# Two gate tiles taken from the attention pools' buffers, and the T4 products of the first two column blocks put ahead of both T1 products

## The chip, the cores and the metric

The kernel runs on one core of a Trainium2 chip. A core has a matrix engine (TensorE: PE in the profile, and PEld for its weight loads), VectorE (DVE), ScalarE (ACT), GpSimd (POOL) and SyncE (SP), each with its own in-order stream of instructions, and DMA queues that move data between the chip's memory and the on-chip buffers. The metric is the time of one execution of the whole program on the device, in microseconds (us), smaller being better.

## The reference

One block of a hybrid network, batch 1, 1024 tokens, width 1024, all in float32:

```python
mod = jax.nn.silu(c) @ w_mod[l] + b_mod[l]
u = modulate(rms_norm(h, ln1_g[l]), shift1, scale1)
# token_mixer(u):
proj = u @ w_in
p_fox, p_rwkv, p_gate = _split(proj, (FOX_COLS, RWKV_COLS, GATE_COLS))
...   # o_fox: causal attention, 8 heads of 64, with a forget-gate bias on the logits
...   # o_rwkv: a linear recurrence over the tokens, 8 heads of 64
gate_fox, gate_rwkv = jnp.split(jax.nn.sigmoid(p_gate), N_BRANCHES, axis=-1)
merged = gate_fox * (o_fox @ fox_w_out) + gate_rwkv * (o_rwkv @ rwkv_w_out)
mix = merged @ w_o
...
h = h + gate1[:, None, :] * mix
u2 = modulate(rms_norm(h, ln2_g[l]), shift2, scale2)
# conv_ffn(u2):
a, b = jnp.split(u @ w_up, 2, axis=-1)      # 2 x 2816 columns
a = lax.conv_general_dilated(a, ...) + conv_b   # width 3, causal, each channel by itself
h = h + gate2[:, None, :] * ((jax.nn.silu(a) * b) @ w_down)
return rms_norm(h, final_g)
```

The change touches two places of it: `sigmoid(p_gate)`, and the product `u @ w_up`.

## The kernel before

Every product of float32 matrices is made as three products of a faster matrix format (float32r): a high part (ACT rounds the number, a CAST) and a low part (DVE subtracts the high part from it) stand for each operand, and hi·hi, hi·lo and lo·hi are added up in one accumulator bank of 128x512 numbers. There are eight such banks.

The program goes through stages: the modulation and norm, the recurrence (with the projections and most gates woven between its steps), the attention, the two branch products and the output product (`br`, `wo`), the up product, the down product (`D`). On PE the program's text sets the order. On ACT, DVE and SP it is the text's order inside `manual_schedule` stretches (the attention, and the up product from its second tokens' half on); outside them a scheduler orders the instructions by its own estimate of when each can start. So in the recurrence's tail the order on ACT, DVE and SP follows from what the scheduler believes each instruction waits for.

**The gates.** `gate_steps` (L327) works out 128 gate columns for 1024 tokens in two halves of 512. A half is 24 matmuls into a bank `gt`, then on ACT Abs (L337), Exp (L338) and Ln (L339), on DVE one instruction (L340) that reads the bank once more, on ACT Exp (L341), and on SP a store to `d_gate` (L342). Everything works in one buffer `gs`. That buffer comes from the pool `gsp` (tag `sp0`, two buffers, used in turn), so that the Abs of a half must wait until the store of the half before the last has left the buffer. The bank comes from the pool `pb` (tag `big`, two banks, in turn): the bank of a half is free when its L340 is done. The halves of gate 8 are called `gs8_0` and `gs8_1` here, their banks `gt8_0` and `gt8_1`; they are the only ones that stand in the program between the opening of the attention's pools and the attention.

At L987 the pools of the attention open: `at` with the heads' operands (`stA`, `stB`, `vh`, which POOL loads at L995 to L999), the probabilities `P` (four buffers) and the short probabilities `Ps` (two buffers, 128x512, for the first four row blocks of a head), and banks. `load_head(0)` starts the first head's loads. Then `weave.step()` runs what is left of gate 8, and the attention begins. From there a gate goes another way (`late_gate`, L1134): all of its halves share one bank, `rk_ps`, which is the second of the two next banks of `pb`; a half is 24 matmuls, then Abs (L1162) and Relu (L1163) on ACT, after which the bank is free for the next half's matmuls. In the program's order `rk_ps` takes the bank that `gt8_0` had. Gate 9's first half comes right behind `gt8_1` on PE, gate 9's second half is interleaved with the first logits `lg`.

**The up product.** It is made for blocks i of 128 columns of each of the two parts (22 of them), by a scheme with seven half-size products instead of eight. Product k of block i, (i, k) below, multiplies one combination of weights by one combination of tokens, 12 matmuls:

```python
OPS = {1: ("A11", "B11"), 2: ("A12", "B21"), 3: ("S4", "B22"), 4: ("A22", "T4"), 5: ("S1", "T1"), 6: ("S2", "T2"),
       7: ("S3", "T3")}
```

Products 1, 6, 5, 3 of a block accumulate in one bank `X`, products 7 and 4 in a bank `Y`. What a bank holds in between is used too: after (i, 4) DVE adds `Y` to `U` (L1564), after (i, 5) it adds `X` to `Z` (L1566, into `Ze_a` for the first two blocks), and only then may (i, 3) go on in `X`. The list `plan` is the order of the products on PE, and also the order in which `up_ahead` makes the weights' operands (a CAST at L1481 and a subtraction at L1485 each), four to six products ahead. The tokens' combinations are made in between, in the text's order: T2 behind the first four products, then T4 (L1750), T1 (L1754) and the high and low parts of B22 (L1722, L1724), each combination as four casts and four subtractions of 128x512. The sums for S4 stand at L1477, two instructions before S4's subtraction on DVE. What the products leave is fetched by `up_evac`, called in the order of `plan`.

Of the kernel before, what the change touches and what calls it, by code (L numbers as in the profile page):

```python
# [9 lines left out]
F32 = mybir.dt.float32  # L10
# [8 lines left out]
NH = 512  # L19
# [113 lines left out]
def hybrid_block(ctx: ExitStack, tc: tile.TileContext, a, out):  # L133
# [110 lines left out]
    marks = {}  # L244
# [40 lines left out]
    def gemm_steps(ps, w, x, cs, nk=KT, w0=0, by_kt=False):  # L285
        (wh, wl), (xh, xl) = w, x
        order = [(i, kt) for i in range(3) for kt in range(nk)]
        if by_kt:
            order.sort(key=lambda o: o[1])
        for n, (i, kt) in enumerate(order):  # L290
            ww, xx = ((wh, xh), (wh, xl), (wl, xh))[i]
            k0 = (w0 + kt) * 128
            mm(ps, ww[:, k0 : k0 + 128], xx[:, kt, cs], start=n == 0, stop=n == len(order) - 1)
            yield
# [32 lines left out]
    def gate_steps(w, i, pps, ptag, pool, tag):  # L327
        if weave.late == 1:
            yield from late_gate(w, i)
            return  # L330
        for hf in range(2):
            cs = slice(hf * NH, hf * NH + NH)
            ps = pps.tile([128, NH], F32, tag=ptag, name=f"gt{i}_{hf}")
            yield from gemm_steps(ps, w, u, cs)

            g = pool.tile([128, NH], F32, tag=tag, name=f"gs{i}_{hf}")
            nc.scalar.activation(g, ps, AF.Abs)  # L337
            nc.scalar.activation(g, g, AF.Exp, scale=-1.0)  # L338
            nc.scalar.activation(g, g, AF.Ln, bias=1.0)  # L339
            stt(g, ps, 0.0, g, op0=ALU.min, op1=ALU.subtract)  # L340
            nc.scalar.activation(g, g, AF.Exp)  # L341
            nc.sync.dma_start(d_gate[i, :, cs], g)  # L342
# [3 lines left out]
    with ExitStack() as es:  # L346
# [613 lines left out]
        for i in range(16):  # L960
            weave.add(lambda i=i: w_in(26 + i), lambda w, i=i: gate_steps(w, i, pb, "big", gsp, "sp0"))
# [26 lines left out]
    at = es.enter_context(tc.tile_pool(name="at", bufs=2, reuse_waits="tile"))  # L988
# [4 lines left out]
    def load_head(h):  # L993
        A = at.tile([128, 2, S], F32R, tag="stA", name=f"stA{h}")
        nc.gpsimd.dma_start(A, d_st[h, 0:2, :, :].rearrange("k r s -> r k s"))  # L995
        B = at.tile([128, 2, S], F32R, tag="stB", name=f"stB{h}")
        nc.gpsimd.dma_start(B[0:68, :, :], d_st[h, 2:4, 0:68, :].rearrange("k r s -> r k s"))
        vh = at.tile([128, 8, 128], F32R, tag="vh", name=f"vh{h}")
        i = nc.gpsimd.dma_start(vh, d_v[h])  # L999
        marks.setdefault("head", i)  # L1000
        heads[h] = A, B, vh

    load_head(0)
    while len(weave.queue) > 12:
        weave.step()
    fx = [[fxp.tile([128, S], F32R, tag=f"h{4 * x + p}", name=f"fx{x}{p}") for p in range(4)] for x in range(2)]
# [3 lines left out]
    with tc.manual_schedule(engines={mybir.EngineType.DVE, mybir.EngineType.Activation}):  # L1010
# [129 lines left out]
        def late_gate(w, i):  # L1140
            while any(x[1] is w[1] for x in late_lo):
                for _ in lower():
                    pass
            for hf in range(2):
                cs = slice(hf * NH, hf * NH + NH)
                yield from gemm_steps(rk_ps, w, u, cs)
                if i == 15 and hf == 1:

                    marks["rest"] = rk_ps
                    return  # L1150
                weave.hold = weave.now + 1000
                pending.append((i, hf))
                weave.spawn(gate_out(i, hf, cs), 260)
                yield
# [76 lines left out]
    if "rest" in marks:  # L1231
        g, m = (gsp.tile([128, NH], F32, tag="sp0", name=f"rest{k}") for k in range(2))
        i = nc.scalar.activation(g, marks["rest"], AF.Abs)
# [89 lines left out]
    for x in range(2):  # L1323
        for n in range(8):
            if x or n:
                k = 8 * x + n + 1
# [277 lines left out]
        put(6, s1[:, NH:])  # L1604

    plan = [(i, k) for ks in ((1, 2), (7,), (6,)) for i in range(2) for k in ks]
    plan += [(0, 4), (0, 5), (1, 5), (1, 4), (0, 3), (1, 3)] + [(2, k) for k in (1, 7, 6, 2, 4, 5)]
    for i in range(3, NFF):
        plan += [(i, 1), (i, 7), (i - 1, 3)] + [(i, k) for k in ((6, 2, 4, 5) if i < NFF - 1 else (6, 2, 5, 4))]
    plan.append((NFF - 1, 3))  # L1610
# [427 lines left out]
```

## Time and profile before

| | us |
|---|---|
| median of 3 runs | 1646.45 (1645.22 to 1648.16) |
| the profiled execution | 1648.91, its span 1647.1 |
| PE busy | 1607.8 (98% of the span) |
| DVE busy | 1222.6 (74%) |
| ACT busy | 820.9 (50%) |
| POOL busy | 130.8 (8%) |

The span is the time from the first to the last recorded instruction; the execution's own time is 1.8 us more. A row of the timeline has the start, the duration, the engine, the line, what is written and what is read, the shapes and the count of merged instructions, and in brackets how long the engine had been idle and whom it waited for. A matmul's recorded duration (0.39 us) is longer than the distance to the next one (0.227 us), since they overlap. The stage borders used below: the attention starts at about 622 us, the up product at about 1000 us, its regular part at 1054 us, the down product at 1430 us.

### The profile page before, as it was taken

The page shows a single profiled execution, that of the slowest core. Times are in us where ns is not written, and L with a number is a line of the kernel's source. Part 1 is how long each engine was busy: PE and PEld are TensorE (multiplying, and loading weights), DVE is VectorE, ACT ScalarE, POOL GpSimd, SP SyncE. Part 2 cuts the span into 40 slices and gives each one's busy share as a digit, 9 for nine tenths or more (in the row PEclk, how much of TensorE's full clock was granted, in tenths as well). Part 3 has the DMA queues.
Part 4 walks back from the last instruction along what each step waited for, and adds up shares of the span by engine and source line. Part 5 has one row for each costly group of instructions (what it writes and reads, how often), then busy time and mean ns, then how long its engine had stood idle before and what let it go on. Part 6 is the DMA issues. An engine that isn't in the chain of part 4 may idle for free.

```text
span 1647.1 us, 25947 instructions
## 1 busy us (share of the span) xinstructions
PE 1607.8 (98%) x9694; PEld 1339.6 (81%) x9694; DVE 1222.6 (74%) x2373; ACT 820.9 (50%) x1537; POOL 130.8 (8%) x153
## 2 busy tenths in 40 slices
PE   7999999999999999999999999999999999999998
PEld 7777788798978788888888888788888888888886
DVE  5786787878876526888679447887777777886677
ACT  5563335445445646766623235644444444555455
POOL 0011101111111010221022000000000000000000
PEclk9999999999999999999999999999999999999999
DMA  8488645543332346433197420242232232675363
GB/s 339 138 326 242 178 123 143 134 123 94 107 115 85 97 126 157 129 117 106 56 353 270 168 81 26 84 134 97 96 119 98 96 109 96 225 254 160 122 211 109
DMA packets 121645, 240.59 MB, mean 146 GB/s; under 512 B 40048, under 2 KB 48880, under 8 KB 121520
## 3 DMA queue, kind: packets, MB, share of 16 engines
q1 hardware_dynamic: 113040, 220.58, 41.0%
q0 software_dynamic: 8480, 18.37, 4.2%
q8 instruction: 76, 1.25, 0.3%
q14 instruction: 49, 0.40, 0.1%
HBM read 173.35 MB, written 65.54 MB: 145 GB/s over the span
## 4 chain that ended last, share of the span: by engine, by line
PE 58%; DVE 5%; ACT 2%; DMA 2%; issue 1%; SPq 0%; ACTq 0%; DVEq 0%
PE X L141 13%; PE D L141 13%; PE Y L141 6%; PE wo L141 5%; PE br L141 4%; PE rk_ps L141 3%; PE W L141 3%; PE gt L141 3%; PE lg L141 2%; PE ov L141 2%; PE tp L145 2%; DMA d_gate<-gs 1%; DVE nm L1049 1%; DVE P L1059 1%; DVE tl L1089 0%
## 5 line engine op out<-in xcount | busy, mean ns | idle before, releaser
L141 PE MATMUL D<-op,op 128*128 128x512 f32 x924 | 209.8, 389 | 0.0
L141 PEld LDWEIGHTS D<-op,op 128*128 128x128 f32 x924 | 173.3, 188 | 36.3 <-DVE op L1261 0.3
L141 PE MATMUL X<-T_m,S 128*128 128x512 f32 x440 | 107.8, 390 | 1.6 <-ACT T_m L1722 1.1
L141 PEld LDWEIGHTS X<-T_m,S 128*128 128x128 f32 x440 | 82.4, 188 | 20.4 <-ACT T_m L1722 2.5
L1260 ACT CAST op<-g 128x512 fp32r<-128x512 f32 x77 | 47.8, 621 | 73.8 <-PE D L141 49.0
L1261 DVE TENSOR_TENSOR op<-g,op 128x512 fp32r<-128x512 f32 x77 | 53.0, 688 | 41.4 <-ACT op L1260 41.4
L1519 DVE SCALAR_TENSOR_TENSOR c<-ab,vec,c 128x512 f32<-128x512 f32 x88 | 65.9, 750 | 18.4 <-ACT c L1522 16.8
L784 DVE TENSOR_TENSOR t<-E,M 128x60 f32<-128x60 f32 (+24 forms) x248 | 55.6, 224 | 27.9 <-DMA M<-sm 21.8
L1485 DVE TENSOR_TENSOR A<-ur,A 128x512 fp32r<-128x512 f32 x64 | 44.0, 688 | 38.7 <-ACT A L1481 38.5
L1485 DVE TENSOR_TENSOR S<-ur,S 128x512 fp32r<-128x512 f32 x66 | 45.5, 691 | 35.2 <-ACT S L1481 35.1
L274 DVE TENSOR_TENSOR lo_in<-raw_in,hi_in 128x512 fp32r<-128x512 f32 x84 | 56.7, 712 | 17.6 <-PE gt L141 4.8
L1481 ACT CAST S<-ur 128x512 fp32r<-128x512 f32 x66 | 41.0, 622 | 55.8 <-DVE ur L1474 30.6
L141 PE MATMUL Y<-T_h,S 128*128 128x512 f32 x264 | 63.6, 390 | 0.4 <-ACT T_h L1740 0.4
L141 PE MATMUL Y<-T_h,A 128*128 128x512 f32 x264 | 63.7, 389 | 0.3 <-ACT T_h L1722 0.3
L1053 ACT ACTIVATE P<-lg,nm 128x896 f32<-128x896 f32 (+3 forms) x64 | 47.4, 743 | 30.7 <-DVE nm L1049 22.5
L1481 ACT CAST A<-ur 128x512 fp32r<-128x512 f32 x64 | 39.6, 622 | 43.1 <-PE X L141 31.3
L786 DVE TENSOR_TENSOR E<-E,t 128x60 f32<-128x60 f32 (+24 forms) x248 | 56.2, 227 | 6.4
L141 PE MATMUL W<-B_f,A 128*128 128x512 f32 x252 | 60.6, 389 | 0.0
L141 PE MATMUL X<-B_b,A 128*128 128x512 f32 x252 | 60.5, 389 | 0.0
L141 PEld LDWEIGHTS Y<-T_h,S 128*128 128x128 f32 x264 | 49.5, 188 | 11.1 <-ACT T_h L1740 0.8
L141 PEld LDWEIGHTS Y<-T_h,A 128*128 128x128 f32 x264 | 49.5, 188 | 10.9 <-ACT T_h L1722 0.7
L272 ACT CAST hi_in<-raw_in 128x1024 fp32r<-128x1024 f32 x42 | 43.8, 1048 | 26.3 <-PE ps_rkv L141 11.3
(483 smaller groups left out, 4134.4 us busy)
## 6 DMA issues: line engine op xcount, KB each, us to landing
raw_in<-in_w_in SPq DMA_DIRECT2D x50, 512.0 KB, 4.0
wm<-in_w_mod SPq DMA_DIRECT2D x48, 512.0 KB, 7.3
ur<-in_w_up SPq DMA_DIRECT2D x44, 512.0 KB, 3.8
g<-d_g SPq DMA_DIRECT2D x35, 512.0 KB, 4.0
d_g<-gs SPq DMA_DIRECT2D x44, 256.0 KB, 2.0
d_g<-c SPq DMA_DIRECT2D x33, 256.0 KB, 4.4
d_st<-qh SPq DMA_DIRECT2D x64, 128.0 KB, 2.5
stA<-d_st POOLq DMA_DIRECT2D x8, 1024.0 KB, 6.9
```

The source lines that it names most:

```text
L141: nc.tensor.matmul(o, lhsT, rhs, start=start, stop=stop, skip_group_check=more)
L145: nc.tensor.transpose(o, i, eye)
L272: nc.scalar.copy(hi, raw)
L274: nc.vector.tensor_tensor(lo[:, c : c + NH], raw[:, c : c + NH], f32(hi[:, c : c + NH]), op=ALU.subtract)
L784: tt(tv, E32[:, 0:J, s : s + 1].to_broadcast([128, J, W]), M32[:, s : s + 1, s + 1 : 32].to_broadcast([128, J, W]), op=ALU.mult)
L786: tt(E32[:, 0:J, s + 1 : 32], E32[:, 0:J, s + 1 : 32], tv, op=ALU.add)
L1053: nc.scalar.activation(e[:, 0:n], lg[:, 0:n], AF.Exp, bias=nm[:, 0:1], accum_out=nm[:, 1:2])
L1260: nc.scalar.copy(hi, src)
L1261: tt(lo, src, f32(hi), op=ALU.subtract)
L1481: nc.scalar.copy(hi, src)
L1485: tt(lo, src, f32(hi), op=ALU.subtract)
L1519: stt(c, ab[:, x + hf * NH : x + hf * NH + NH], V("conv_w", 22 * x + i), c, op0=ALU.mult, op1=ALU.add)
```

## The change

Three lines of code move. A gate's buffer `gs` comes from the attention's pool, tag `Ps`, if that pool is open (only the two halves of gate 8 meet this). And in the list `plan` the product (1, 4) moves from behind (1, 5) to a place right behind (0, 4).

```diff
@@ gate_steps
-            g = pool.tile([128, NH], F32, tag=tag, name=f"gs{i}_{hf}")
+            g = marks["spare"].tile([128, NH], F32, tag="Ps", name=f"gs{i}_{hf}", bufs=2) if "spare" in marks else \
+                pool.tile([128, NH], F32, tag=tag, name=f"gs{i}_{hf}")
             nc.scalar.activation(g, ps, AF.Abs)
             nc.scalar.activation(g, g, AF.Exp, scale=-1.0)
             nc.scalar.activation(g, g, AF.Ln, bias=1.0)
...
     load_head(0)
+    marks["spare"] = at
     while len(weave.queue) > 12:
         weave.step()
...
-    plan += [(0, 4), (0, 5), (1, 5), (1, 4), (0, 3), (1, 3)] + [(2, k) for k in (1, 7, 6, 2, 4, 5)]
+    plan += [(0, 4), (1, 4), (0, 5), (1, 5), (0, 3), (1, 3)] + [(2, k) for k in (1, 7, 6, 2, 4, 5)]
```

Line numbers below L337 are one larger in the changed kernel from L337 on, and two larger from L1005 on.

The first place is ACT at the end of the recurrence. The scheduler orders ACT there, and with other buffers it chose another order. Before, the rows for gate 8, with the last normalisation of the recurrence (`rs`) in them:

```order
L337 ACTIVATE gs8_0_6850<-gt8_0_6777 128x512
L932 ACTIVATE rs3_1_6811<-va3_1_6786,epsr_76 128x512
L338 ACTIVATE gs8_0_6850<-gs8_0_6850 128x512
L933 ACTIVATE rs3_1_6811<-rs3_1_6811 128x512
L339 ACTIVATE gs8_0_6850<-gs8_0_6850 128x512
L341 ACTIVATE gs8_0_6850<-gs8_0_6850 128x512
L337 ACTIVATE gs8_1_6882<-gt8_1_6857 128x512
L338 ACTIVATE gs8_1_6882<-gs8_1_6882 128x512
L339 ACTIVATE gs8_1_6882<-gs8_1_6882 128x512
L341 ACTIVATE gs8_1_6882<-gs8_1_6882 128x512
L1162 ACTIVATE gs9_0_6922<-rk_ps_6892 128x512
```

And the same stretch of ACT in the changed kernel:

```order
L933 ACTIVATE rs3_1_6811<-va3_1_6786,epsr_76 128x512
L934 ACTIVATE rs3_1_6811<-rs3_1_6811 128x512
L338 ACTIVATE gs8_0_6850<-gt8_0_6777 128x512
L338 ACTIVATE gs8_1_6882<-gt8_1_6857 128x512
L339 ACTIVATE gs8_0_6850<-gs8_0_6850 128x512
L339 ACTIVATE gs8_1_6882<-gs8_1_6882 128x512
L340 ACTIVATE gs8_0_6850<-gs8_0_6850 128x512
L340 ACTIVATE gs8_1_6882<-gs8_1_6882 128x512
L342 ACTIVATE gs8_0_6850<-gs8_0_6850 128x512
L342 ACTIVATE gs8_1_6882<-gs8_1_6882 128x512
L1164 ACTIVATE gs9_0_6922<-rk_ps_6892 128x512
```

The two halves, which stood one behind the other, are now interleaved step by step: the Abs of the second half, which reads the bank `gt8_1`, stands ahead of the Exp of the first. On DVE the L340 of `gs8_0` moves behind the recurrence's last two instructions accordingly, and on SP the store of `gs8_0` moves behind the recurrence's last store. PE's order there is the same in both. The first two `Ps` probabilities now stand behind gate 8's two stores, since they use the same two buffers.

The second place is DVE in the up product, between the low parts of B22 (whose second half is the first row) and the fetch of (1, 4) or (1, 5). Before:

```order
L1724 TENSOR_TENSOR B221_m13_10937<-u21_m11_10666,B220_e3_10935 128x512 x2
L1485 TENSOR_TENSOR A22_1_10946<-ur11_10422,A22_1_10946 128x512
L1566 TENSOR_TENSOR Ze_a7_10662<-X_0_10678,Ze_a7_10662 128x512
L1477 TENSOR_TENSOR ur00_10309<-ur00_10309 128x512
L1485 TENSOR_TENSOR S4_0_10963<-ur00_10309,S4_0_10963 128x512
L1566 TENSOR_TENSOR Ze_a7_10662<-X_1_10750,Ze_a7_10662 128x512
L1477 TENSOR_TENSOR ur10_10421<-ur10_10421 128x512
L1485 TENSOR_TENSOR S4_1_10984<-ur10_10421,S4_1_10984 128x512
L1485 TENSOR_TENSOR A11_2_10986<-ur20_10966,A11_2_10986 128x512
L1564 TENSOR_TENSOR U_1_10900<-Y_1_10841,U_1_10900 128x512
```

And in the changed kernel:

```order
L1726 TENSOR_TENSOR B221_m13_10937<-u21_m11_10666,B220_e3_10935 128x512 x2
L1487 TENSOR_TENSOR S1_1_10946<-ur11_10422,S1_1_10946 128x512
L1566 TENSOR_TENSOR U_1_10900<-Y_1_10841,U_1_10900 128x512
L1479 TENSOR_TENSOR ur00_10309<-ur00_10309 128x512
L1487 TENSOR_TENSOR S4_0_10963<-ur00_10309,S4_0_10963 128x512
L1568 TENSOR_TENSOR Ze_a7_10662<-X_0_10678,Ze_a7_10662 128x512
L1479 TENSOR_TENSOR ur10_10421<-ur10_10421 128x512
L1487 TENSOR_TENSOR S4_1_10984<-ur10_10421,S4_1_10984 128x512
L1487 TENSOR_TENSOR A11_2_10986<-ur20_10966,A11_2_10986 128x512
L1568 TENSOR_TENSOR Ze_a7_10662<-X_1_10750,Ze_a7_10662 128x512
```

The three fetches have moved in a circle: the fetch of (1, 4), which stood last, now stands first, and the two fetches into `Ze_a` ((0, 5) and (1, 5)) stand one fetch later, each behind a sum and a low part for S4. The operands S1 of both blocks are made one place later and A22 of block 1 two places earlier, on ACT as on DVE.

## The prediction

> **What bounds the kernel now.** First the page's heads, then the chain that ended last, in order of time.
>
> ```profile
> span 1647.1 us, 25947 instructions
> PE 1607.8 (98%) x9694; PEld 1339.6 (81%) x9694; DVE 1222.6 (74%) x2373; ACT 820.9 (50%) x1537; POOL 130.8 (8%) x153
> ```
> ```profile
> 607.50 10.46 DMA d_gate<-gs
> ...
> 622.39 6.21 PE rk_ps L141 x19
> ...
> 1054.26 3.04 PE X L141 x12
> ...
> 1429.94 209.68 PE D L141 x924
> ```
>
> PE is busy for 98%, so only its few gaps can be won or lost. From 1054.26 us on the chain is PE alone, to the end: what PE is late by there, the program is late by. One long piece ahead of that isn't PE: a gate store of 10.46 us. The timeline around it (gate 8, then gate 9 in `rk_ps`):
>
> ```profile
> 609.14 0.60 ACT L337 ACTIVATE gs<-gt 128x512 f32<-128x512 f32 x1 [1.66 <-PE gt L141]
> 609.63 0.68 ACT L932 ACTIVATE rs<-va,epsr 128x512 f32<-128x512 f32 x1
> ...
> 612.05 0.68 DVE L340 SCALAR_TENSOR_TENSOR gs<-gt,gs 128x512 f32<-128x512 f32 x1
> ...
> 613.04 1.98 PE L141 MATMUL gt<-u_hi,lo_in 128*128 128x512 f32 x8
> ...
> 614.85 1.98 PE L141 MATMUL rk_ps<-u_hi,hi_in 128*128 128x512 f32 x8
> ...
> 618.05 0.60 ACT L337 ACTIVATE gs<-gt 128x512 f32<-128x512 f32 x1 [4.64 <-DMA d_gate<-gs]
> ...
> 618.48 1.98 PE L141 MATMUL rk_ps<-u_hi,lo_in 128*128 128x512 f32 x8
> ...
> 618.68 0.63 ACT L338 ACTIVATE gs<-gs 128x512 f32<-128x512 f32 x1
> ...
> 621.27 0.58 ACT L1162 ACTIVATE gs<-rk_ps 128x512 f32<-128x512 f32 x1
> ...
> 621.74 0.59 ACT L1163 ACTIVATE gm<-rk_ps 128x512 f32<-128x512 f32 x1
> ...
> 622.39 3.33 PE L141 MATMUL rk_ps<-u_hi,hi_in 128*128 128x512 f32 x8 [1.93 <-ACT gm L1163]
> ...
> 627.75 0.85 PE L141 MATMUL rk_ps<-u_hi,lo_in 128*128 128x512 f32 x3
> ```
>
> The Abs of `gs8_1` (618.05) waits for the store to leave its buffer; behind it on ACT stand the Abs and Relu of `rk_ps`, and for these PE waits 1.93 us (620.46 to 622.39). Look at 614.85 too: `rk_ps` starts without a gap, since the L340 of `gs8_0` (612.05 to 612.73) has left its bank in time.
>
> **The gate tile, step by step.** It removes the wait for the store, no instruction. It also reorders ACT: the Abs of `gs8_1` now stands ahead of the Exp of `gs8_0`. That Abs reads `gt8_1`, which PE ends at 613.04 + 1.98 = 615.02. ACT is in order, so the rest of `gs8_0` waits for it, and with it L340, and with L340 the bank that `rk_ps` needs. With a distance of 0.49 to 0.52 us between ACT instructions (609.14 to 609.63) and 0.03 per hand-over: Abs of `gs8_1` at 615.06, Exp 615.57, Exp 616.08, Ln of `gs8_0` 616.60 to 617.22, L340 617.25 to 617.93, `rk_ps` at 617.97. PE begins it 3.12 us later than at 614.85. Its 24 matmuls take 618.48 + 1.98 − 614.85 = 5.61 (0.40 for the last, 0.227 from one to the next), to 623.58. ACT is free by then (the last Exp of `gs8_1` ends near 619.3), so Abs and Relu follow at 623.62 and 624.11, the Relu ends at 624.70, and the second half starts at 624.76 instead of 622.39: **+2.37 us**. The gap has moved from behind `rk_ps`' first half to ahead of it and grown: 1.93 before, 2.95 + 1.18 = 4.13 now.
>
> Does the attention pass this on? Its first logits stand behind these matmuls on PE and everything in it hangs on them; the two reused buffers and the reordered stores aren't late (below). I take all of 2.37; the other end is 0, if some transfer with a fixed time were what the attention waits for.
>
> DMA: the store of `gs8_0` is issued at about 618.65 instead of 613.4, the store of `gs8_1` at 619.3 instead of 621.4, the recurrence's last store is no longer behind a gate's on SP. The first two short probabilities now wait for these two stores:
>
> ```profile
> 635.02 0.36 ACT L1053 ACTIVATE P<-lg,nm 128x128 f32<-128x128 f32 x1
> ```
> ```profile
> vh<-d_v POOLq DMA_DIRECT2D x1, 512.0 KB, 20.5
> ```
>
> They would be written at 635.02 + 2.37 = 637.4, so a store may take 18 us. The store above took 10.46 amid the heads' loads; the slowest row there (20.5) is of twice the size. I take 0; the other end is 20.5 − 18 = 2.5 us.
>
> **The clock.** The timeline has eight matmuls in 3.33 us at 622.39, against 1.98 elsewhere. Stretches of 3.41 us show why:
>
> ```profile
> 619.53:622.94 3.41, 1.48 (x7) 0.91 (x6) 0.69 (x1) 2.62 (x6) 0.00 (x0) 1.00 1.35 285
> 622.94:626.36 3.42, 3.42 (x9) 2.67 (x8) 1.90 (x3) 1.21 (x2) 0.00 (x0) 0.50 1.20 213
> 674.15:677.56 3.41, 1.68 (x15) 1.68 (x15) 3.31 (x7) 3.38 (x7) 0.00 (x0) 1.00 0.62 117
> 677.56:680.97 3.41, 3.41 (x28) 3.22 (x28) 3.24 (x8) 2.58 (x9) 0.96 (x2) 1.00 0.46 151
> ```
>
> (The second column is PE's busy time, the third from the end the granted clock.) Behind a stretch in which PE was busy for 1.48 of 3.41 us the clock is 0.50 for one stretch; behind one with 1.68 it stays 1.00. So some 1.8 us idle in one stretch decide. The price: the 19 matmuls end at 627.75 + 0.85 = 628.60, 6.21 us behind their start, where 18 × 0.227 + 0.40 = 4.49 would do: 1.7 us. If the stretches fall anywhere on the program, a gap of 1.93 lies whole in one in (3.41 − 1.93) / 3.41 = 43% of the runs. A gap of 2.95 leaves 1.9 or more in one stretch unless a border cuts it between 1.05 and 1.90 us, 25% of the runs: 75%; and a second slow stretch can follow, since 1.18 idle come right behind. I put the half clock at 0.43 × 1.7 = 0.75 us on average before, and at 0.75 × 1.7 = 1.3 with 0.45 for a second stretch after: **+1.0 us** (from 0, where both have it or neither, to 3.4, two stretches against none).
>
> The Trainium skill, page "TensorE: Matmul & The Clock Gate", section "Part 1: The HAM clock gate", says that the clock halves after a whole idle window of about 3.4 us in a grid that runs freely. Here a window that was 43% busy was enough, so the trace has a lower bar than the page. By the page a gap of 2.95 us would never slow PE, and the sum would lack the +1.0.
>
> **T4 ahead of T1, step by step.** The same work, no instruction more. The rows of the first two blocks before:
>
> ```profile
> 1030.13 2.33 PE L141 MATMUL Y<-T_h,A 128*128 128x512 f32 x9 [0.28 <-ACT T_h L1722]
> ...
> 1033.36 1.02 PE L141 MATMUL X<-T_m,S 128*128 128x512 f32 x2 [0.90 <-ACT T_m L1722]
> ...
> 1034.94 0.62 ACT L1481 CAST S<-ur 128x512 fp32r<-128x512 f32 x1
> ...
> 1036.13 0.68 DVE L1485 TENSOR_TENSOR S<-ur,S 128x512 fp32r<-128x512 f32 x1
> ...
> 1039.74 0.68 DVE L1485 TENSOR_TENSOR A<-ur,A 128x512 fp32r<-128x512 f32 x1
> 1039.98 2.88 PE L141 MATMUL Y<-T_h,A 128*128 128x512 f32 x12
> 1040.35 0.68 DVE L1566 TENSOR_TENSOR Ze_a<-X,Ze_a 128x512 f32<-128x512 f32 x1
> 1040.95 0.68 DVE L1477 TENSOR_TENSOR ur<-ur 128x512 f32<-128x512 f32 x1
> 1041.66 0.62 ACT L1481 CAST S<-ur 128x512 fp32r<-128x512 f32 x1 [3.50 <-DVE ur L1477]
> 1042.31 0.69 DVE L1485 TENSOR_TENSOR S<-ur,S 128x512 fp32r<-128x512 f32 x1 [0.69 <-ACT S L1481]
> ...
> 1042.70 1.98 PE L141 MATMUL X<-B_e,S 128*128 128x512 f32 x8
> ...
> 1045.42 1.98 PE L141 MATMUL X<-B_e,S 128*128 128x512 f32 x8
> 1045.50 0.68 DVE L1485 TENSOR_TENSOR A<-ur,A 128x512 fp32r<-128x512 f32 x1
> ...
> 1054.26 3.04 PE L141 MATMUL X<-T_m,S 128*128 128x512 f32 x12 [0.52 <-ACT x L1559]
> ```
>
> A product takes 2.72 us (1039.98 to 1042.70). (0, 4) could hand over at 1030.13 + 9 × 0.227 = 1032.17, but (0, 5) starts at 1033.36 and stumbles over T1's casts until 1037.26 (1039.98 − 2.72): 5.09 us for 2.72, 2.37 us of stalls. Now (1, 4) fills 1032.17 to 1034.89. The operands keep their slots on ACT and DVE, with other contents:
> - (0, 5): S1's cast is in the slot that ends at 1035.56, its low part in the one that ends at 1036.81. Start 1035.60, second four matmuls at 1036.83, end 1038.64.
> - (1, 5): its low part is in the slot 1039.74 to 1040.42, so its second four wait until 1040.44; end 1042.25. The two blocks stand 0.45 us ahead of before.
> - (0, 3) writes on in the bank `X` that `Ze_a` must first read. That read stood at 1040.35; now it stands behind the S4 sum, its cast and its low part: 1043.00 to 1043.60. Start 1043.63, not 1042.70.
> - (1, 3): its read stands behind the low part of A11 now (1045.50 to 1046.18), so 1046.10 to 1046.78. Start 1046.81, not 1045.42: 1.39 late.
>
> Then three products without a wait: (2, 6) at 1046.81 + 3 × 2.72 = 1054.97, where it stood at 1054.26, behind a wait of 0.52 for ACT that hides the rest. **+0.71 us**. The other ends: +1.39, if the 0.52 stays as well, and −2.37, if every stall is filled and no new one comes. The chain of this stretch speaks against a gain, though: between 1031 and 1054 it runs over DVE, whose work is the same in both.
>
> ```profile
> 1031.40 1.98 DVE uf_e L1754 x4
> ...
> 1037.42 2.40 DVE B_m L1724 x4
> ```
>
> **Sum**: 2.37 + 1.0 + 0.71 = +4.1 us. The profiled execution (1648.91, span 1647.1) is 2.5 above the median and had a half-clock stretch; with the clock's term as an average I add to the median: 1646.45 + 4.1 = **1650.5 us**.
>
> **The rivals** (0.2%, or 3.3 us, is about what a measurement of this kernel tells from no change.)
> - *A, the sum*: 0.64; 1648.5 to 1653.5.
> - *B, the store's wait was what mattered*: if the L340 of `gs8_0` still ends before 614.85, `rk_ps` starts as before, ACT has `gs8_1` done by 618.9, its Abs and Relu of `rk_ps` run from 620.5 to 621.6 and the second half starts there: −0.8, and no half clock: −0.75. 1644.9, not slower; with T1's stalls filled too, 1642.9. For it speaks the 4.64 us row, against it ACT's order. It decides at one instruction, the Abs ahead of the Exp. 0.08, half of it over 0.2% faster.
> - *C, the gate loses, the up product gains*: 3.37 − 2.0, 1647.8. For it: 2.37 us of stalls stand in the rows; against: the new reads behind S4, and DVE as the bound. 0.04.
> - *D, the attention takes up the late start*: 0.71 alone, 1647.2. For it: ACT and DVE work lies on the path there; against: that work starts from PE. 0.10.
> - *E, a store holds up the first short probabilities*: up to 2.5 more, 1653. 0.05.
> - *F, the clock stays full after the change*: 2.37 + 0.71 − 0.75 = +2.3, 1648.8. For it: the border between 1.48 and 1.68 rests on two rows; against: 2.95 us idle are well beyond it. By the page's rule named above it would come out so, and the trace's 0.50 behind a 43% window disagrees. 0.09.
>
> The range leaves out B and the far ends of E and A: 1646.8 to 1654.0. Faster by over 0.2%: half of B, 0.04. Within: the rest of B, C, D, F and the 0.08 of A below 1649.7, 0.35. Slower: 0.61.
>
> **What would show it.** In the changed kernel's timeline: ACT's Abs of `gs8_1` near 615.1 and no wait for `d_gate`; a PE gap of some 3 us ahead of `rk_ps`, a second of 1.2 behind its first half, half clock near them; (1, 4) in place of the stall at 1032; new gaps ahead of (0, 3) and (1, 3), put down to `Ze_a`. Wrong would be: `rk_ps` without a gap, or an attention that ends less than 2 us later.

## The result and the profile after

The change makes the kernel slower, by about as much as forecast. Beside six runs of the kernel before (median 1647.69 us, 1645.22 to 1650.09; three of the six are those on whose median the forecast stands), six runs of the changed kernel have a median of 1653.49 us (1652.77 to 1655.31): a ratio of 1.0033, with a 95% interval of 1.0023 to 1.0043. Between the medians these are 5.8 us, where 4.1 were forecast. The time lies inside the range of 1646.8 to 1654.0, near its upper end, and 3.0 us above the 1650.5 forecast: 1.7 us of that are the larger difference, the rest is a kernel before that ran slower than in the forecast's three runs.

The head of the changed kernel's page (its own time is 1653.13 us), and some pieces of its chain of work in order of time:

```profile
span 1651.4 us, 25951 instructions
PE 1608.7 (97%) x9694; PEld 1339.5 (81%) x9694; DVE 1224.7 (74%) x2373; ACT 821.1 (50%) x1537; POOL 130.8 (8%) x153
```
```profile
609.96 5.47 PE gt L141 x24
616.05 1.03 ACT gs L339 x2
618.38 5.77 PE rk_ps L141 x24
625.31 4.61 PE rk_ps L141 x19
```

PE has the same 9694 matmuls and is busy about as long; the added time is idle time of PE. The store of the gate (10.46 us) has left this place of the chain, and ACT's steps for gate 8 stand in it instead. The timeline of the changed kernel there (start, duration, then the wait ahead of it and what ended the wait; a line of the code stands one further down than before, and two behind the second edit):

```profile
613.44 1.98 PE L141 MATMUL gt<-u_hi,lo_in 128*128 128x512 f32 x8
615.45 0.60 ACT L338 ACTIVATE gs<-gt 128x512 f32<-128x512 f32 x1 [3.61 <-PE gt L141]
615.95 1.14 ACT L339 ACTIVATE gs<-gs 128x512 f32<-128x512 f32 x2
616.98 1.14 ACT L340 ACTIVATE gs<-gs 128x512 f32<-128x512 f32 x2
617.63 1.29 DVE L341 SCALAR_TENSOR_TENSOR gs<-gt,gs 128x512 f32<-128x512 f32 x2 [3.91 <-ACT gs L340]
618.38 2.12 PE L141 MATMUL rk_ps<-u_hi,hi_in 128*128 128x512 f32 x8 [2.96 <-DVE gs L341]
624.17 0.60 ACT L1164 ACTIVATE gs<-rk_ps 128x512 f32<-128x512 f32 x1 [4.58 <-PE rk_ps L141]
624.66 0.59 ACT L1165 ACTIVATE gm<-rk_ps 128x512 f32<-128x512 f32 x1
625.31 2.11 PE L141 MATMUL rk_ps<-u_hi,hi_in 128*128 128x512 f32 x8 [1.18 <-ACT gm L1165]
```

ACT waits 3.61 us, for PE's last matmul into `gt8_1` and no longer for `d_gate`; behind it stand the Exp and Ln of both halves in pairs, and PE waits 2.96 us ahead of `rk_ps` and 1.18 behind its first half. In the up product:

```profile
1033.57 5.06 PE L141 MATMUL Y<-T_h,A 128*128 128x512 f32 x21 [0.27 <-ACT T_h L1724]
1039.06 2.46 PE L141 MATMUL X<-T_m,S 128*128 128x512 f32 x8 [0.42 <-ACT S L1483]
1043.93 1.19 PE L141 MATMUL X<-T_m,S 128*128 128x512 f32 x4 [0.57 <-DVE S L1487]
1046.36 0.68 DVE L1568 TENSOR_TENSOR Ze_a<-X,Ze_a 128x512 f32<-128x512 f32 x1
1047.19 2.09 PE L141 MATMUL X<-B_e,S 128*128 128x512 f32 x8 [1.16 <-DVE Ze_a L1568]
1050.37 2.09 PE L141 MATMUL X<-B_e,S 128*128 128x512 f32 x8 [0.18 <-DVE Ze_a L1568]
```

The first row is the end of (0, 4) and the whole of (1, 4), without a stall between them. Then (0, 5), the part of (1, 5) behind its wait, (0, 3) and (1, 3) stand here in this order, the last two with a wait for the reads into `Ze_a`.

The program from the last matmul of gate 8 on, cut at the same instructions of PE in every kernel (us from start to start; the first row holds the gap in question; the kernels of the other columns are described below):

| | before | after | tile alone | plan alone | tile, old ACT order | plan, reads first |
|---|---|---|---|---|---|---|
| last matmul of gate 8 to second half of `rk_ps` | 7.76 | 10.28 | 10.27 | 10.06 | 7.00 | 7.00 |
| from there to the first logits | 6.05 | 4.44 | 4.44 | 6.69 | 4.44 | 4.44 |
| first logits to first `br` | 191.97 | 193.49 | 193.40 | 191.98 | 193.39 | 191.89 |
| first `br` to first `wo` | 88.09 | 88.71 | 88.31 | 88.49 | 88.38 | 88.16 |
| first `wo` to first `D` | 521.28 | 522.06 | 521.27 | 522.06 | 521.26 | 521.28 |
| first `D` to last `D` | 209.44 | 209.44 | 209.44 | 209.43 | 209.40 | 209.40 |

The last matmul of gate 8 itself starts between 614.6 and 618.0 us in these executions, in no order that follows the edits, so spans are not compared, but stages. The stage from `br` to `wo` differs by up to 0.6 us, in no such order either: the second execution of the change has 88.29 us there.

### The profile page after: what moved, and what is told of

It is laid out like the page before. It is cut to its first block, busy times and chain, and to the rows that moved or that the text cites. A ratio compares the mean times of both kernels' runs of the same rounds, so it can differ in the third digit from the quotient of the medians.

```text
span 1651.4 us, 25951 instructions
## 1 busy us (share of the span) xinstructions
PE 1608.7 (97%) x9694; PEld 1339.5 (81%) x9694; DVE 1224.7 (74%) x2373; ACT 821.1 (50%) x1537; POOL 130.8 (8%) x153
## 4 chain that ended last, share of the span: by engine, by line
PE 60%; DVE 5%; ACT 2%; DMA 1%; issue 1%; SPq 0%; ACTq 0%; DVEq 0%
PE X L141 13%; PE D L141 13%; PE Y L141 7%; PE wo L141 5%; PE br L141 4%; PE gt L141 4%; PE rk_ps L141 4%; PE W L141 3%; PE lg L141 2%; PE ov L141 2%; PE tp L145 2%; DVE P L1061 1%; DVE nm L1051 1%; DVE tl L1091 0%; DMA d_gate<-rest 0%
```

## The experiments

Eight kernels, in two groups; within a group all ran on one chip, beside 35 runs of the kernel before (median 1649.72 us) in the first group and 31 (1649.99) in the second. The ratios are to the kernel before, each with its 95% interval; they are not quotients of the medians, and can differ from these in the last digits.

**Each part alone.** The tile without the plan:

```diff
-    plan += [(0, 4), (1, 4), (0, 5), (1, 5), (0, 3), (1, 3)] + ...
+    plan += [(0, 4), (0, 5), (1, 5), (1, 4), (0, 3), (1, 3)] + ...
```

> Only the gate tile's change, the products' order as before. Theory (the reordered ACT work holds the bank that rk_ps needs): +2.4 us from the later start of rk_ps' second half and about +1 us of half clock on average, 2.4 to 5 us over the kernel before; ACT's order as in the changed kernel, a PE gap of 2.96 us ahead of rk_ps, none of it waiting for d_gate. Rival (the wait for the store was what mattered): 0.8 to 1.6 us faster than before. Rival (the attention takes up a late start): within 0.5 us of before.

The plan without the tile:

```diff
-            g = marks["spare"].tile([128, NH], F32, tag="Ps", name=f"gs{i}_{hf}", bufs=2) if "spare" in marks else \
-                pool.tile([128, NH], F32, tag=tag, name=f"gs{i}_{hf}")
+            g = pool.tile([128, NH], F32, tag=tag, name=f"gs{i}_{hf}")
...
-    marks["spare"] = at
```

> Only the move of the product (1, 4), the gates' tile as before. Theory (the reads into Ze_a now stand behind the S4 operands on DVE): +0.7 to +1.0 us; gaps ahead of (0, 3) of some 1.2 us and ahead of (1, 3), put down to Ze_a, and (2, 6) 0.7 to 1.0 us later behind the start of (0, 4). Rival (T1's stalls are filled and nothing new comes): -2.0 us.

The tile alone: 1653.57 us, 1.0021 (1.0012 to 1.0031). The plan alone: 1651.58 us, 1.0014 (1.0002 to 1.0027). Both cost, and 1.0021 times 1.0014 is 1.0035. In the table, the plan's price stands in one row only (first `wo` to first `D`, +0.78 to +0.80) and is the same with and without the tile. The times are coarser than that: 1.0002 to 1.0027 are 0.3 to 4.5 us, so they barely say that the plan costs; the row says how much.

The execution of the plan alone showed something that neither theory had foreseen. The gate's code in it is that of the kernel before, yet its rows at the gate are worse than there:

```profile
622.50 0.60 ACT L337 ACTIVATE gs<-gt 128x512 f32<-128x512 f32 x1 [6.94 <-DMA d_gate<-gs]
626.84 3.78 PE L141 MATMUL rk_ps<-u_hi,hi_in 128*128 128x512 f32 x8 [4.23 <-ACT gm L1163]
```

ACT waited 6.94 us for the store where it had waited 4.64, and PE 4.23 us where it had waited 1.93. So what the tile takes away is no fixed wait but one that differs from execution to execution.

**The tile with ACT's old order.** The same buffers as in the change, but the Abs of `gs8_1` is held behind the last Exp of `gs8_0` in the order that the scheduler writes (an edge without a wait), and the plan is that of before:

```diff
-            nc.scalar.activation(g, ps, AF.Abs)
+            first = nc.scalar.activation(g, ps, AF.Abs)
+            if "half" in marks:
+                tc.add_manual_dep(first.ins, marks["half"].ins.name, NOSYNC)
...
-            nc.scalar.activation(g, g, AF.Exp)
+            final = nc.scalar.activation(g, g, AF.Exp)
+            if "spare" in marks:
+                marks["half"] = final
```

> The gate tile's change alone, and the second half of gate 8 kept behind the first on ACT, as before the change; the same buffers and addresses as with the tile alone. Theory (ACT's order is the cause): rk_ps starts without a gap behind gate 8, its second half some 0.8 us earlier than in the kernel before, no half clock there: 0.8 to 1.6 us faster than before, and 3.2 to 6 us faster than the tile alone. Rival (the buffers' place, or the short probabilities waiting for the stores): as slow as the tile alone.

1649.56 us, 0.9995 (0.9985 to 1.0005): 4.0 us below the tile alone, with the same two buffers. That it is faster than the kernel before, as was expected, is not shown. Rows of PE and ACT in it:

```profile
616.83 1.98 PE L141 MATMUL rk_ps<-u_hi,hi_in 128*128 128x512 f32 x8
617.02 0.60 ACT L338 ACTIVATE gs<-gt 128x512 f32<-128x512 f32 x1 [0.48 <-PE gt L141]
623.60 2.11 PE L141 MATMUL rk_ps<-u_hi,hi_in 128*128 128x512 f32 x8 [1.17 <-ACT gm L1169]
```

`rk_ps` starts without a gap, ACT waits 0.48 us for PE alone, and the second half stands 7.00 us behind the last matmul of gate 8 instead of 10.27. The price of the tile at the gate is thus shown to be the place of one instruction on ACT and of what follows it, 3.27 us; the buffers themselves cost nothing that these runs can tell. (Only the order of gate 8's two halves is the old one: the two steps of `rs` stand ahead of them, as in the changed kernel.)

**The plan with the reads ahead of S4's sums.** The plan of the change, the gate of before, and one or two products less of lead for the weights' operands, so that on DVE the reads into `Ze_a` come first:

```diff
-            lower = up_ahead(done["run"] + (4 if done["run"] < 7 else 3 if done["run"] < 11 else 4 if ...
+            lower = up_ahead(done["run"] + (4 if done["run"] < 7 else 3 if done["run"] < 10
+                                            else 2 if done["run"] < 12 else 3 if done["run"] < 13 else 4 if ...
```

> The move of (1, 4) alone, and the weights' operands made one product later around it, so that the two reads into Ze_a stand ahead of the sums for S4 on DVE. Theory (those reads are what (0, 3) and (1, 3) wait for, and DVE's work, which is the same, sets the end of this stretch): (0, 3) starts at most 0.3 us later than in the kernel before, the time is within 0.4 us of before. Rival (PE's stalls set the end): 1 to 2 us faster than before. Rival (something else than the reads costs): +0.7 to +1.0 us as with the plan alone.

1649.27 us, 0.9997 (0.9986 to 1.0008). The stage takes 521.28 us, as before the change. (0, 3) and (1, 3) now wait for something else, shorter; in the rows of this kernel:

```profile
1041.98 0.68 DVE L1566 TENSOR_TENSOR Ze_a<-X,Ze_a 128x512 f32<-128x512 f32 x1
1043.95 0.69 DVE L1485 TENSOR_TENSOR S<-ur,S 128x512 fp32r<-128x512 f32 x1 [0.69 <-ACT S L1481]
1043.97 2.14 PE L141 MATMUL X<-B_e,S 128*128 128x512 f32 x8 [0.34 <-ACT S L1481]
1044.56 0.69 DVE L1566 TENSOR_TENSOR Ze_a<-X,Ze_a 128x512 f32<-128x512 f32 x1
```

The read ends at 1042.66, and PE starts (0, 3) at 1043.97 behind S4's cast. So the late reads are the plan's price: with them early it is gone. Nothing is won either, for the products now wait for operands from DVE and ACT. That no order could win anything here isn't shown, since this edit itself makes these operands later.

**The change once more, and with its gap filled.** The second group has the changed kernel unaltered, and with 12 matmuls, whose result nobody reads, ahead of `rk_ps`:

> The changed kernel once more, beside the kernels that follow. If its parts add, 1.0021 for the tile alone and 1.0014 for the plan alone make 1.0035 of before, 5.8 us. If half a clock near the gap ahead of rk_ps is part of its price in some executions, its profile may show a half-rate stretch between 616 and 628 us, which the first profile did not show; the times would then spread by 1.5 to 1.7 us.

```diff
+    warm = pt.tile([128, NH], F32, tag="tp", name="warm")
+    for n in range(12):
+        nc.tensor.matmul(warm, u_hi[:, 0, 0:128], u_hi[:, 0, 0:NH], start=n == 0, stop=n == 11)
```

> The changed kernel with 12 products that nobody reads, put on TensorE ahead of the first product into rk_ps, where it stands idle for 2.96 us (12 at 0.215 us are 2.58 us). They add work and no output changes. If the clock is the price of this gap (1.0 us in the mean, as forecast), this runs 1 us faster than the change in the same company, about 1.0027 of before. If the wait alone is the price, it runs as the change does, 1.0033, since the second half of rk_ps still waits for the same ScalarE steps: 10.3 us between the last gate product and the second half of rk_ps. If the products themselves get in the way, it is slower by up to 0.5 us.

The change: 1654.32 us, 1.0027 (1.0015 to 1.0039). With the gap filled: 1653.38 us, 1.0024 (1.0015 to 1.0033). The profile of the second execution of the change has what the first lacked. In all these profiles the granted clock changes only at the borders of a grid of 3.41 us (in the second execution it is halved at 617.51 and full again at 624.34, two steps later). First the stretches between such borders around the gap in the first execution, then in the second (second column PE's busy time; third from the end the granted clock):

```profile
613.28:616.69 3.41, 2.13 (x10) 1.44 (x8) 0.45 (x1) 1.24 (x3) 3.02 (x4) 1.00 1.32 316
616.69:620.11 3.42, 1.73 (x8) 1.42 (x8) 1.29 (x2) 2.66 (x5) 0.23 (x1) 1.00 1.21 288
620.11:623.52 3.41, 3.41 (x16) 2.82 (x15) 0.00 (x0) 0.00 (x0) 0.00 (x0) 1.00 1.32 208
```
```profile
614.10:617.51 3.41, 1.42 (x7) 0.84 (x5) 0.20 (x1) 1.96 (x4) 3.31 (x4) 1.00 1.04 301
617.51:620.92 3.41, 2.44 (x6) 1.96 (x7) 1.29 (x2) 1.94 (x4) 0.00 (x0) 0.50 1.23 291
620.92:624.34 3.42, 3.42 (x10) 2.65 (x9) 0.00 (x0) 0.00 (x0) 0.00 (x0) 0.50 1.30 202
```

The gap is 2.96 us in both. In the first a border cut it, no stretch had less than 1.73 us of work, and the clock stayed full. In the second one stretch had 1.42 us, and two at half clock followed: the second half of `rk_ps` comes 13.01 us behind the last matmul of gate 8 instead of 10.28, so the two cost 2.73 us. With the gap filled no half clock stands there, and the second half comes after 10.31 us:

```profile
617.24 2.88 PE L1012 MATMUL warm<-u_hi 128*128 128x512 f32 x12
620.37 2.14 PE L141 MATMUL rk_ps<-u_hi,hi_in 128*128 128x512 f32 x8 [0.25 <-DVE gs L341]
```
```profile
616.32:619.73 3.41, 3.41 (x17) 2.82 (x15) 1.03 (x2) 2.30 (x5) 2.58 (x4) 1.00 1.17 225
```

Gate 8's last matmul ends at 617.40 in this execution. Without the extra matmuls the stretch from 616.32 on would have had 1.1 us of work (an estimate, 617.40 less 616.32), less than any here that left the clock full. So here they kept the clock full, and removed none of the wait. The runs with the gap filled average 1.2 us below those of the change, with an interval of 0.3 to 2.3 worked out by drawing the runs of both again; the two ratios' intervals overlap widely, so the size of the clock's part is known no better than that.

**Both mended.** The old order on ACT and the early reads together, under the change's buffers and plan:

> Both parts of the change, the tile with the old order on ScalarE and the plan with the reads into Ze_a ahead of the sums of S4. If the two causes are the whole, nothing of the change's price is left: 7.0 us between the last gate product and the second half of rk_ps, 400.8 us between the output product and the first D, and 0.999 of before (0.9995 and 0.9997 of the two alone), some 5.5 us below the change. If the tile has a price of its own later (the half-rate stretch near 676 us, seen with all three kernels that have the tile and with none of the three without), the stretch stands in this profile too and 1.5 us are left: 1.0003 of before.

1649.11 us, 0.9993 (0.9983 to 1.0004), 5.2 us below the change between the medians of the same group. The stages are 7.00 and 4.44 us at the gate and 521.27 us from `wo` to `D`. This kernel may be 1 us better than the one before, but the interval includes no change at all. Its profile does have the half-clock stretch near 676 us (from first logits to first `br` 193.6 us).

**The next head's loads later**, in the kernel before:

```diff
-                if k % 4 == 1 and h < 7:
+                if k % 4 == (3 if h == 0 else 1) and h < 7:
                     load_head(h + 1)
```

> The kernel before, with the loads of the second head (2 MB on the POOL queue) issued two blocks of rows later. In the kernel before they are issued at 614.3 us, while the store of the gate's first half is still on its way (issued at 607.5, landed at 618.0). If they hold up the store, it lands sooner, the wait of ScalarE (4.64 us) shrinks by about 2 us or is gone, 7.0 us stand between the last gate product and the second half of rk_ps, and the kernel is 1 to 3 us faster than before, 0.999. If the first head's loads (issued at 606.2 to 608 us) hold it up, it lands after 9 to 13 us as before and the time stays within 0.1%.

1650.66 us, 1.0007 (0.9996 to 1.0018): not faster. But the edit didn't move the loads. The first of the next head's loads, in the kernel before and in this one:

```profile
614.26 0.70 POOL L995 DMA_DIRECT2D stA<-d_st  x1
```
```profile
614.75 0.70 POOL L995 DMA_DIRECT2D stA<-d_st  x1
```

Each is issued 0.37 us before the last matmul of gate 8 starts (614.63 and 615.12). The recorded instructions stand in the same order on all engines of the two kernels. So the times test nothing about the loads, and the run is in effect the kernel before once more. (The store in question, issued at 607.50 in the kernel before, is that of gate 7's second half, whose buffer `gs8_1` takes over.) In its profile the wait for the store is shorter (2.60 us instead of 4.64), and 7.00 us stand at the gate; the plan with the reads first, whose gate is also that of before, had 3.39 and 7.00. What makes the store slow, the loads or something else, is left open.

This profile does settle another point. In the profile of the change and those of the first group, every kernel with the tile had a half-clock stretch near 676 us, and none without it. Here is the same in a kernel without the tile:

```profile
670.92:674.33 3.41, 1.44 (x9) 0.93 (x8) 3.28 (x8) 3.10 (x7) 0.00 (x0) 1.00 0.79 176
674.33:677.74 3.41, 3.41 (x19) 3.41 (x18) 2.93 (x6) 2.38 (x5) 0.00 (x0) 0.50 0.28 102
```

while the second execution of the change, which has the tile, has none (191.83 us from first logits to first `br`; its 1.96 us of idle time, near 678 us, are cut by a border), nor has the one with the gap filled. So the stretch belongs to a gap of 1.95 to 1.98 us that all kernels have there, and to where the grid happens to lie.

## Why the prediction was right, point by point

**The gate tile: right, step by step.** The last matmul of gate 8 starts 0.40 us later in the profile after than in that before; with this added, the forecast was 615.46 for the Abs of `gs8_1` and 618.37 for `rk_ps`. The rows have 615.45 and 618.38. The second half was due at 625.16 and came at 625.31, so that the term is 2.52 us (10.28 less 7.76) where 2.37 stood. Nearly all of the 0.15 lies in the first eight matmuls behind the gap, which take 2.12 us here and 1.98 where no gap is ahead of them. That the order on ACT does it, and not the buffers, the run with the old order showed.

**What the term stood against: only half right.** The 2.37 us took the kernel before's wait for the store as it was in one execution, 1.93 us of PE's time. The four executions whose gate is that of before had the second half of `rk_ps` after 7.00 (twice), 7.76 and 10.06 us. The changed kernel's 10.28 has no store in it; so the difference is anything from 0.2 to 3.3 us by the execution that one compares with. That the one that the forecast read lies near the mean of the four (7.96 us) was luck. The times agree: every kernel whose gate waits for the store has a standard deviation of 1.7 to 2.7 us in its runs (the kernel before 2.0 and 2.2), every one with the tile, in either order on ACT, 0.75 to 1.6.

**The clock: the mechanism right, the mean not measurable.** The forecast put half the clock at 75% of the executions of the change, with a second slow stretch in some. Of the three profiled executions with the 2.96 us gap (the change twice, the tile alone), one had it, with two stretches; two had a border in the gap, at 1.73 us of work or more. The price per stretch was near (2.73 us for two, where 1.7 stood for one), and that some 1.8 us idle decide was right: stretches with 1.42 to 1.48 us of work were followed by half the clock, while that with 1.73 us, shown further up, was not, nor was this one with 1.61 in the run with the reads first, whose clock stayed full to 1645 us:

```profile
187.86:191.27 3.41, 1.61 (x9) 0.98 (x7) 3.34 (x10) 1.32 (x2) 0.00 (x0) 1.00 0.67 172
```

The Trainium skill, page "TensorE: Matmul & The Clock Gate", section "Part 1: The HAM clock gate", asks for a wholly idle window; the second execution of the change, with a window 42% busy, disagrees again. The kernel before is not free of half the clock either: its profile lost 1.6 us to one stretch behind the gap (6.05 against 4.44 us) and the plan alone 2.25 to two. Whether the change has more of it in the mean than the kernel before, the forecast's +1.0, three or four executions on each side cannot tell. Filling the gap gained 1.2 us (0.3 to 2.3), which is the whole of the change's part and not its excess.

**The up product: right but for one detail.** +0.71 us was forecast, +0.78 measured. With the later start of the stage taken off (3.46 us, by the first `wo`), (0, 5) was due at 1035.60 and came at 1035.60; (0, 3) was due at 1043.63 and came at 1043.73; (1, 3) at 1046.81 against 1046.91. Then the three products without a wait take 0.13 us more than forecast, since the matmuls behind a wait again run late (2.09 us for eight), and (2, 6) starts 0.94 us late (1058.66); in the kernel before, (2, 6) itself stands behind a wait and takes 0.16 longer, which leaves 0.78. (1, 4) filled the place of T1's stalls, but, as the forecast had it, most of the 2.37 us went to waits for the operands of (0, 5) and (1, 5): (0, 5) starts 0.72 us behind the end of (1, 4), and the two take 3.22 and 3.59 us instead of 2.72. So 0.3 us were left (0.45 in the forecast), and the reads cost these and more. That DVE's and ACT's chain bounds this stretch fits the run with the reads first, which took 521.28 us, the same as before; as said there, it isn't shown by that run alone.

**The rivals.** *B* (the store's wait was what mattered) fell: its condition, L340 of `gs8_0` in time for `rk_ps`, did not hold. With ACT's old order it does hold, and there the kernel runs at 0.9995, so B had named the right deciding instruction; its gain of some 1.5 us over the kernel before is not shown. *C* (the up product gains) fell. *D* (the attention takes up the late start) fell: from the first logits to the first `br` the second execution of the change needs 191.83 us, the kernel before 191.97, so a later start is passed on whole. *E* (a store holds up the first short probabilities) was not seen: the first one in the changed kernel starts without a wait.

```profile
636.34 0.36 ACT L1055 ACTIVATE P<-lg,nm 128x128 f32<-128x128 f32 x1
```

*F* (the clock stays full) is what the first execution did near the gap, and not the second.

**The sum.** Against the kernel with both mended, the accounts close as far as they are known: 3.28 us for the order on ACT, 0.79 for the reads and 1.2 (0.3 to 2.3) for the clock behind the gap make 5.3, and 5.2 were measured. Against the kernel before, whose own waits vary, the medians differ by 5.8 us in one comparison and 4.3 in the other, and the two intervals (3.8 to 7.1 us and 2.5 to 6.4) both hold the 4.1 of the forecast. The first comparison's higher figure rests on six runs of a kernel whose runs spread over 8 to 10 us; no trace shows a term for it. The forecast also stood on a median of three runs, 1646.45, where 35 and 31 later runs of the same kernel on other occasions gave 1649.72 and 1649.99. That the time lies in the forecast's range is therefore partly luck: on the second occasion the change's median, 1654.32, lay above 1654.0. What held is the difference and where it comes from, not the absolute time.

## What to carry to other kernels

Freeing a buffer changes more than a wait: where a scheduler writes the order, an instruction that no longer seems to wait moves ahead of others on an in-order engine, and if it still has another input to wait for, all that it overtook waits with it. Look at what the overtaken work releases (here an accumulator bank), and if the buffer is wanted, hold the order and take only the buffer. And a transfer's wait read from one execution is one draw: where it stands against a fixed cost, ask for its spread before the difference is taken. An edit of the program's text need not move anything where a scheduler writes the order: look in the trace whether it did.

## What was not expected of the hardware

A store of 256 KB beside the loads of a head landed, by the wait that it ended, 8.5, 9.3, 10.5 and 12.8 us after its issue in four executions whose instructions stand in the same order up to there (616.50 less 608.01, 620.21 less 610.93, 617.96 less 607.50, 622.50 less 609.67). And a kernel of one core can have a half-clock stretch or not at the same gap of the same program: near 676 us a gap of 1.95 to 1.98 us, which all have, cost 1.5 to 1.7 us in five of ten profiled executions (two of the change, one of every other kernel) and nothing in the other five, by where the grid's border fell.
